# A two-layer hybrid encoder on one core: how its norms are cut, ordered and queued

## The chip, the core and the metric

The kernel runs on one NeuronCore of a Trainium2 chip. The core has five engines with a queue of instructions each: TensorE (PE: matmuls and transposes, with its weight loads listed as PEld), VectorE (DVE), ScalarE (ACT), GpSimd (POOL) and SyncE (SP, which here only issues DMAs). Each engine takes its own instructions in a fixed order; semaphores hold an instruction back until what it reads is written. SBUF is the working memory, PSUM holds what PE writes, in banks of 512 fp32 columns. The metric is the time of one execution on the device, in microseconds (us).

## The reference

A sequence of 256 tokens with 1024 features goes through two layers and a final RMSNorm, all in float32. Each layer is

```
mod = silu(c) @ ada_w + ada_b                 -> sh_m, sc_m, g_m, sh_f, sc_f, g_f
h   = rms_norm(x, norm_mix_g) * (1 + sc_m) + sh_m
proj = h @ w_in                               -> three attention branches and three gates
merged = sigmoid(ga) * (o_na @ w_br_na) + sigmoid(gb) * (o_mla @ w_br_mla) + sigmoid(gc) * (o_gqa @ w_br_gqa)
x   = x + g_m * (merged @ w_out)
h   = rms_norm(x, norm_ffn_g) * (1 + sc_f) + sh_f
gate, up = split(h @ ffn_w_gate_up)
x   = x + g_f * ((silu(gate) * up) @ ffn_w_down)
```

with `rms_norm(x, g) = x * rsqrt(mean(x*x) + 1e-6) * g`. The branches are a neighbourhood attention, a latent attention (its query projection is w_uq) and a grouped-query attention.

## The kernel before, in words

**Tiles.** The 256 tokens are two tiles of 128 (t = 0 and 1). Weights stream from HBM; every matmul has a 128x128 block of the transposed activation as its stationary operand and up to 512 columns of a weight as its moving one.

**Two parts.** An fp32 value is split into a rounded part (hi, or whi for weights) and a residual (lo, wlo). `split_to` (L186) does it: ACT casts to the rounded part (L187), DVE subtracts it from the source (L188). A product is then three matmuls: hi x whi (L268), hi x wlo (L269) and lo x whi (L270).

**Items.** The program's work on PE is a list of items. An item is 256 rows of a weight (two chunks of 128, `nk` = 2) and 512 columns or fewer; `load_split` (L241) loads it on SP and splits it on ACT and DVE, into one of seven pairs of split weights (`spl`) through one of five raw buffers (`rawp`). Its matmuls are six for each tile. `group` (L254) makes the items of one weight slice: the first opens a PSUM accumulation, the last one's `post` function reads the sum.

**Order.** The main loop (L902) goes through the items. The first twelve run both tiles at once, in regions that fix PE's order as written (L918). From then on tile 0 runs an item as soon as it comes, and tile 1 follows LAG = 4 items behind, out of the list `pend` (L926). At the places in `flush` all of tile 1's pending items run before the list goes on, as the following stage needs the complete row of x. `step` (L896) counts the executed items; `later(k, f)` runs f that many steps later, and so puts PE's transposes behind other matmuls. `side` holds other work for given items: loads and sums for `mod` (L143), biases, attention.

Within an engine the order is not wholly that of the program text: a planner orders ready instructions by priority, and priority is by default the place in the text.

**A norm.** There are three such places: before each layer's FFN (`iF`, one per layer) and before the second layer's projection (`i0`). `post_res` (L696) takes half a row (cg = 0 or 1, 512 columns) of one tile: DVE multiplies the sum by the gate (L702) and adds it to x (L703), ACT sums the squares (L192). After the second half `norm` (L223) follows for that tile: `x_rstd` (L195) adds the two sums and EPS on POOL (L197) and raises to the power -0.5, also on POOL (L108); `x_scaled` (L200) scales both halves of x on DVE (L202). DN = 4 steps later the deferred part runs: `transposed` (L205) transposes four chunks of 128 columns into one PSUM bank (L209), and `modulate` (L212) makes of each chunk `A * x + B` on ACT (L218), then the rounded part on ACT (L187) and the residual on DVE (L188). The next stage's matmuls of that tile read them as hi and lo. The first norm of all is another function, `first_x` (L825), with the same `x_rstd`; after the last layer `after_ffn` (L770) uses `x_rstd` and writes the output.

Of the kernel before, what the change touches and what calls it, by code (L numbers as in the profile page):

```python
# [15 lines left out]
P = 128  # L16
# [10 lines left out]
LAG = 4  # L27
# [5 lines left out]
DN = 4  # L33
# [3 lines left out]
def encoder_kernel(ctx: ExitStack, tc: tile.TileContext, x, consts, cols, rows, ada_b, rpb, ada_w, w_in,  # L37
# [152 lines left out]
    def sumsq(t, hf, ss):  # L190
        junk = t2([P, 512])
        nc.scalar.activation(junk, x_sb[:, t, hf * 512:(hf + 1) * 512], AF.Square, scale=1.0 / 32.0,  # L192
                             accum_out=ss[:, hf:hf + 1])

    def x_rstd(t, ss):  # L195
        ms = sm(1)
        nc.gpsimd.tensor_scalar(out=ms, in0=ss[:, 0:1], scalar1=ss[:, 1:2], scalar2=EPS, op0=ALU.add, op1=ALU.add)  # L197
        return rstd_of(ms, 1)
# [13 lines left out]
    def modulate(t, kc0, n, xT, A, B, hT):  # L212
        full = t2([P, 512])
        fv = full.rearrange("p (j q) -> p j q", j=4)
        for j in range(n + 1):
            if j < n:
                kc = kc0 + j
                nc.scalar.activation(fv[:, j, :], xT[:, j, :], AF.Identity, scale=A[:, kc:kc + 1], bias=B[:, kc:kc + 1])  # L218
            if j >= 1:
                kc = kc0 + j - 1  # L220
                split_to(hT[0][:, kc, t * P:(t + 1) * P], hT[1][:, kc, t * P:(t + 1) * P], fv[:, j - 1, :])

    def norm(t, ss, A, B, hT):  # L223
        r = x_rstd(t, ss)
        xs = [x_scaled(t, r, hf) for hf in range(2)]

        def b_():
            for hf in range(2):
                modulate(t, hf * 4, 4, transposed(xs[hf]), A, B, hT)
# [24 lines left out]
    def group(units_src, nkc, n, lhs, post, bank=None):  # L254
# [3 lines left out]
        for u in range(nu):  # L258
            nk = min(2, nkc - 2 * u)

            def mm(t, it, u=u, nk=nk):
# [3 lines left out]
                for j in range(nk):  # L265
                    kc = 2 * u + j
                    first, last = kc == 0, kc == nkc - 1
                    nc.tensor.matmul(ps[t][:, 0:n], lhs(t, 0, kc), hi[:, j, 0:n], start=first, stop=False)  # L268
                    nc.tensor.matmul(ps[t][:, 0:n], lhs(t, 0, kc), lo[:, j, 0:n], start=False, stop=False)  # L269
                    nc.tensor.matmul(ps[t][:, 0:n], lhs(t, 1, kc), hi[:, j, 0:n], start=False, stop=last)  # L270
# [13 lines left out]
    flush = set()  # L284
    cur = [0]
# [18 lines left out]
    def new_ss(key):  # L304
        ssn[key] = {t: smp.tile([P, 2], F32, tag="ss", name=nm("ss")) for t in range(NT)}
# [3 lines left out]
    def layer(l):  # L309
# [341 lines left out]
        flush.add(i0)  # L651
        at(i0 + (7 if l == 0 else 0), params)
# [43 lines left out]
        def post_res(key, m, after, half=None):  # L696
            def f_(cg):
                def f(t, ps):
# [3 lines left out]
                    nc.vector.tensor_tensor(out=y, in0=ps, in1=G, op=ALU.mult)  # L702
                    nc.vector.tensor_tensor(out=xa, in0=xa, in1=y, op=ALU.add)  # L703
                    if key not in ssn:
                        new_ss(key)
                    sumsq(t, cg, ssn[key][t])
# [17 lines left out]
        flush.add(iF)  # L724

# [98 lines left out]

    def first_x():  # L825
# [76 lines left out]
    for i, it in enumerate(items):  # L902
# [10 lines left out]
        if i < 12:  # L913
# [4 lines left out]
            with tc.manual_schedule(engines={mybir.EngineType.PE}):  # L918
# [7 lines left out]
        if len(pend) >= LAG:  # L926
# [74 lines left out]
```

## Time and profile before

| what | us |
|---|---|
| median of 3 runs | 822.37 (821.83 to 822.97) |
| the profiled execution | 822.51 |
| its span, first to last instruction | 820.4 |
| PE busy | 790.7 |
| DVE busy | 598.8 |
| ACT busy | 453.7 |
| POOL busy | 25.8 |
| mean granted clock of PE | 0.991 |

A view lists what the hardware profiler saw in one execution. A line names the source line, the engine, the operation, what it writes <- what it reads, shapes and a count. Matmuls are pipelined: one is listed with 0.39 us but the next starts before its end, so that the distance of two starts tells the rate. "Idle before" is the time in which the engine did nothing just before, and the name behind the arrow is what it waited for last.

### The profile page before, as it was taken

What the parts mean: (1) busy time and instruction counts of PE and PEld (TensorE: products, weight loads), DVE (VectorE), ACT (ScalarE), POOL (GpSimd) and SP (SyncE); (2) the same over time, 40 slices, a digit from 0 to 9 for tenths busy, and PEclk for the clock granted to TensorE, in tenths of its full rate; (3) what the DMA queues carried; (4) which work ended last, traced back from release to release, by engine and by line L of the source; (5) the groups of instructions that cost most, each with busy time, mean ns of one, the idle gap of its engine ahead of it and who ended that gap; (6) DMA issues with size and microseconds to landing.
All of it is one profiled execution on the core that took longest, in us unless ns stands there. A gap on an engine that the chain in (4) does not pass through costs nothing.

```text
span 820.4 us, 10803 instructions
## 1 busy us (share of the span) xinstructions
PE 790.7 (96%) x3776; PEld 633.4 (77%) x3776; DVE 598.8 (73%) x955; ACT 453.7 (55%) x788; POOL 25.8 (3%) x40
## 2 busy tenths in 40 slices
PE   5998999999999999999999999999999999999996
PEld 3786776788878888888878877777887888888884
DVE  3369898789777888875667699878978666665462
ACT  4365887644485444443466687774448544444441
POOL 1002100000000000000000020000000000000000
PEclk9999999999999999999999999999999999999998
DMA  9979488697667989886874668778765677876631
GB/s 315 359 245 273 131 293 252 198 311 227 194 180 241 322 294 306 276 264 190 210 213 137 180 192 279 222 230 283 250 198 182 219 233 223 259 226 184 182 103 52
DMA packets 113414, 187.20 MB, mean 228 GB/s; under 512 B 14672, under 2 KB 34256, under 8 KB 113360
## 3 DMA queue, kind: packets, MB, share of 16 engines
q1 hardware_dynamic: 113360, 186.51, 73.1%
q8 instruction: 30, 0.49, 0.3%
q14 instruction: 24, 0.20, 0.1%
HBM read 185.44 MB, written 1.05 MB: 227 GB/s over the span
## 4 chain that ended last, share of the span: by engine, by line
issue 49%; PE 31%; DVE 8%; DMA 6%; ACT 4%; POOL 1%; POOLq 0%; DVEq 0%; ACTq 0%
PE mm L268 8%; PE mm L270 8%; PE mm L269 8%; DMA raw<-in_ada_w_dram 6%; DVE wlo L188 2%; DVE acc L140 2%; PE tp L861 1%; POOL sm L108 1%; PE o L629 1%; ACT P L587 1%; ACT tm L218 1%; DVE sm L574 1%; PE tp L209 1%; PE tp L608 1%; PE tp L560 1%
## 5 line engine op out<-in xcount | busy, mean ns | idle before, releaser
L188 DVE TENSOR_TENSOR wlo<-raw,whi 128x1024 fp32r<-128x1024 f32 (+2 forms) x248 | 298.3, 1209 | 115.0 <-ACT whi L187 114.8
L187 ACT CAST whi<-raw 128x1024 fp32r<-128x1024 f32 (+2 forms) x248 | 256.9, 1041 | 221.6 <-PE mm L270 137.1
L268 PE MATMUL mm<-whi,hi 128*128 128x512 f32 (+1 forms) x784 | 314.0, 400 | 1.8 <-ACT hi L882 1.1
L270 PE MATMUL mm<-whi,lo 128*128 128x512 f32 (+1 forms) x784 | 307.1, 392 | 0.2
L269 PE MATMUL mm<-wlo,hi 128*128 128x512 f32 (+1 forms) x784 | 306.1, 390 | 0.5 <-DVE wlo L188 0.4
L268 PEld LDWEIGHTS mm<-whi,hi 128*128 128x128 f32 x784 | 148.1, 189 | 34.7 <-issue 5.7
L270 PEld LDWEIGHTS mm<-whi,lo 128*128 128x128 f32 x784 | 147.7, 188 | 32.8 <-DVE lo L188 1.8
L269 PEld LDWEIGHTS mm<-wlo,hi 128*128 128x128 f32 x784 | 148.3, 189 | 28.9 <-DVE wlo L188 1.7
L140 DVE SCALAR_TENSOR_TENSOR acc<-raw,sc,acc 128x512 f32<-128x512 f32 x140 | 104.9, 749 | 32.2 <-DMA raw<-in_ada_w_dram 30.5
L270 PE MATMUL mm<-whi,s 128*128 128x512 f32 (+1 forms) x188 | 73.3, 390 | 2.4 <-DVE s L188 2.4
L268 PE MATMUL mm<-whi,s 128*128 128x512 f32 (+1 forms) x188 | 74.2, 395 | 0.4 <-ACT s L187 0.4
L269 PE MATMUL mm<-wlo,s 128*128 128x512 f32 (+1 forms) x188 | 73.1, 389 | 0.0
L270 PEld LDWEIGHTS mm<-whi,s 128*128 128x128 f32 x188 | 35.4, 189 | 9.8 <-DVE s L188 2.6
L268 PEld LDWEIGHTS mm<-whi,s 128*128 128x128 f32 x188 | 35.3, 188 | 7.9 <-ACT s L187 0.9
L269 PEld LDWEIGHTS mm<-wlo,s 128*128 128x128 f32 x188 | 35.4, 188 | 6.8
L592 ACT ACTIVATE P<-P,sm 128x256 f32<-128x256 f32 x64 | 29.3, 509 | 5.7 <-DVE sm L590 5.6
L587 ACT ACTIVATE P<-tp,sm,rq 128x256 f32<-128x256 f32 x32 | 17.8, 561 | 15.9 <-DVE sm L584 15.8
L197 POOL TENSOR_SCALAR sm<-ss 128x1 f32<-128x1 f32 x10 | 4.0, 404 | 662.4 <-ACT tm L192 662.4
L218 ACT ACTIVATE tm<-tp,cm,cm 128x128 f32<-128x128 f32 x48 | 21.3, 472 | 6.2 <-PE tp L209 6.2
L108 POOL TENSOR_TENSOR sm<-sm,nhalf 128x1 f32<-128x1 f32 (+2 forms) x22 | 18.4, 835 | 127.1 <-DVE sm L370 65.2
L192 ACT ACTIVATE tm<-x_sb 128x512 f32<-128x512 f32 x20 | 12.6, 632 | 16.8 <-DVE x_sb L703 14.6
L733 DVE TENSOR_TENSOR tm<-tm,mm 128x512 f32<-128x512 f32 (+1 forms) x24 | 15.4, 640 | 8.7 <-PE mm L270 7.1
(157 smaller groups left out, 637.7 us busy)
## 6 DMA issues: line engine op xcount, KB each, us to landing
raw<-in_ada_w_dram SPq DMA_DIRECT2D x80, 512.0 KB, 4.8
raw<-in_w_gu_dram SPq DMA_DIRECT2D x80, 512.0 KB, 4.6
raw<-in_w_in_dram SPq DMA_DIRECT2D x64, 512.0 KB, 4.6
raw<-in_w_dn_dram SPq DMA_DIRECT2D x44, 512.0 KB, 4.8
s<-in_ada_w_dram SPq DMA_DIRECT2D x32, 256.0 KB, 6.7
raw<-in_w_out_dram SPq DMA_DIRECT2D x16, 512.0 KB, 4.9
raw<-in_w_in_dram SPq DMA_DIRECT2D x16, 256.0 KB, 5.0
raw<-in_w_gqa_dram SPq DMA_DIRECT2D x8, 512.0 KB, 5.6
```

What stands on the lines that cost most here:

```text
L108: nc.gpsimd.tensor_tensor(out=r, in0=ms, in1=nhalf[:, 0:n], op=ALU.pow)
L140: nc.vector.scalar_tensor_tensor(out=acc, in0=raw[:, j, :], scalar=sc[:, kc:kc + 1], in1=acc, op0=ALU.mult, op1=ALU.add)
L187: nc.scalar.copy(hi_ap, src)
L188: nc.vector.tensor_tensor(out=lo_ap, in0=src, in1=hi_ap.bitcast(F32), op=ALU.subtract)
L192: nc.scalar.activation(junk, x_sb[:, t, hf * 512:(hf + 1) * 512], AF.Square, scale=1.0 / 32.0, accum_out=ss[:, hf:hf + 1])
L218: nc.scalar.activation(fv[:, j, :], xT[:, j, :], AF.Identity, scale=A[:, kc:kc + 1], bias=B[:, kc:kc + 1])
L268: nc.tensor.matmul(ps[t][:, 0:n], lhs(t, 0, kc), hi[:, j, 0:n], start=first, stop=False)
L269: nc.tensor.matmul(ps[t][:, 0:n], lhs(t, 0, kc), lo[:, j, 0:n], start=False, stop=False)
L270: nc.tensor.matmul(ps[t][:, 0:n], lhs(t, 1, kc), hi[:, j, 0:n], start=False, stop=last)
L587: nc.scalar.activation(pt[:, t, :], src[:, t, :], AF.Exp, bias=nb[:, t:t + 1], scale=scale[t], accum_out=rs[:, t:t + 1])
L592: nc.scalar.activation(pt[:, t, :], pt[:, t, :], AF.Copy, scale=rc[:, t:t + 1])
L733: nc.vector.tensor_tensor(out=hd[:, 0:n], in0=sgv, in1=up, op=ALU.mult)
```

## The change

- `sumsq` adds EPS to the first half's sum on DVE; `x_rstd` then adds the second half's on DVE. POOL keeps the power.
- `modulate`: for the first half (chunks 0 to 3) ACT writes the rounded part straight from the transposes, and DVE computes the same `A * x + B` from the transposes on its own and subtracts. For chunks 4 to 7 ACT computes and casts as before, chunk by chunk.
- The steps of `norm`, of `modulate` and of the second half of `post_res` are given high priority: the planner treats them as if they stood at the start of the program.
- DN goes from 4 to 5, and around the three norms (`norm_at`) tile 1 follows five items behind and not four, from one item before the flush to five after it.
- In `group` the six matmuls of an item and tile run as hi x whi for both chunks, hi x wlo for both, lo x whi for both.
- In the first twelve items `issue_after` queues each region's PE instructions behind the last one before it.

```diff
--- before.py
+++ after.py
@@ -30,7 +30,7 @@
 DH = 10
 DM = 4
 DG = 4
-DN = 4
+DN = 5
 
 
 @with_exitstack
@@ -191,10 +191,12 @@
         junk = t2([P, 512])
         nc.scalar.activation(junk, x_sb[:, t, hf * 512:(hf + 1) * 512], AF.Square, scale=1.0 / 32.0,
                              accum_out=ss[:, hf:hf + 1])
+        if hf == 0:
+            nc.vector.tensor_scalar_add(ss[:, 2:3], ss[:, 0:1], EPS)
 
     def x_rstd(t, ss):
         ms = sm(1)
-        nc.gpsimd.tensor_scalar(out=ms, in0=ss[:, 0:1], scalar1=ss[:, 1:2], scalar2=EPS, op0=ALU.add, op1=ALU.add)
+        nc.vector.tensor_tensor(out=ms, in0=ss[:, 1:2], in1=ss[:, 2:3], op=ALU.add)
         return rstd_of(ms, 1)
 
     def x_scaled(t, r, hf):
@@ -212,21 +214,29 @@
     def modulate(t, kc0, n, xT, A, B, hT):
         full = t2([P, 512])
         fv = full.rearrange("p (j q) -> p j q", j=4)
-        for j in range(n + 1):
-            if j < n:
-                kc = kc0 + j
+        for j in range(n):
+            kc = kc0 + j
+            hi, lo = (hT[p][:, kc, t * P:(t + 1) * P] for p in range(2))
+            if kc0 == 0:
+
+                nc.scalar.activation(hi, xT[:, j, :], AF.Identity, scale=A[:, kc:kc + 1], bias=B[:, kc:kc + 1])
+                nc.vector.tensor_scalar(out=fv[:, j, :], in0=xT[:, j, :], scalar1=A[:, kc:kc + 1],
+                                        scalar2=B[:, kc:kc + 1], op0=ALU.mult, op1=ALU.add)
+            else:
                 nc.scalar.activation(fv[:, j, :], xT[:, j, :], AF.Identity, scale=A[:, kc:kc + 1], bias=B[:, kc:kc + 1])
-            if j >= 1:
-                kc = kc0 + j - 1
-                split_to(hT[0][:, kc, t * P:(t + 1) * P], hT[1][:, kc, t * P:(t + 1) * P], fv[:, j - 1, :])
+                nc.scalar.copy(hi, fv[:, j, :])
+            nc.vector.tensor_tensor(out=lo, in0=fv[:, j, :], in1=hi.bitcast(F32), op=ALU.subtract)
 
     def norm(t, ss, A, B, hT):
-        r = x_rstd(t, ss)
-        xs = [x_scaled(t, r, hf) for hf in range(2)]
+        with tc.high_priority():
+            r = x_rstd(t, ss)
+            xs = [x_scaled(t, r, hf) for hf in range(2)]
 
         def b_():
             for hf in range(2):
-                modulate(t, hf * 4, 4, transposed(xs[hf]), A, B, hT)
+                xT = transposed(xs[hf])
+                with tc.high_priority():
+                    modulate(t, hf * 4, 4, xT, A, B, hT)
 
         later(DN, b_)
 
@@ -262,12 +272,12 @@
                 if u == 0:
                     ps[t] = bank(t) if bank else psmm.tile([P, 512], F32, tag="mm", name=nm("mm"))
                 hi, lo = it["w"]
-                for j in range(nk):
-                    kc = 2 * u + j
-                    first, last = kc == 0, kc == nkc - 1
-                    nc.tensor.matmul(ps[t][:, 0:n], lhs(t, 0, kc), hi[:, j, 0:n], start=first, stop=False)
-                    nc.tensor.matmul(ps[t][:, 0:n], lhs(t, 0, kc), lo[:, j, 0:n], start=False, stop=False)
-                    nc.tensor.matmul(ps[t][:, 0:n], lhs(t, 1, kc), hi[:, j, 0:n], start=False, stop=last)
+
+                for n_, (part, w) in enumerate(((0, hi), (0, lo), (1, hi))):
+                    for j in range(nk):
+                        kc = 2 * u + j
+                        nc.tensor.matmul(ps[t][:, 0:n], lhs(t, part, kc), w[:, j, 0:n], start=(kc == 0 and n_ == 0),
+                                         stop=(kc == nkc - 1 and n_ == 2))
 
             pf = None
             if u == nu - 1:
@@ -282,6 +292,7 @@
 
     side = {}
     flush = set()
+    norm_at = []
     cur = [0]
     deferred = []
 
@@ -302,7 +313,7 @@
     ssn = {}
 
     def new_ss(key):
-        ssn[key] = {t: smp.tile([P, 2], F32, tag="ss", name=nm("ss")) for t in range(NT)}
+        ssn[key] = {t: smp.tile([P, 3], F32, tag="ss", name=nm("ss")) for t in range(NT)}
         return ssn[key]
 
 
@@ -649,6 +660,8 @@
             at(s + (k * span) // nseq, f)
 
         flush.add(i0)
+        if l > 0:
+            norm_at.append(i0)
         at(i0 + (7 if l == 0 else 0), params)
         at(i0 + (12 if l == 0 else 8), na_bias)
 
@@ -699,11 +712,14 @@
                     G = mods[(l, m)][:, cg * 512:(cg + 1) * 512]
                     xa = x_sb[:, t, cg * 512:(cg + 1) * 512]
                     y = t2([P, 512])
-                    nc.vector.tensor_tensor(out=y, in0=ps, in1=G, op=ALU.mult)
-                    nc.vector.tensor_tensor(out=xa, in0=xa, in1=y, op=ALU.add)
                     if key not in ssn:
                         new_ss(key)
-                    sumsq(t, cg, ssn[key][t])
+                    with ExitStack() as pri:
+                        if cg == 1:
+                            pri.enter_context(tc.high_priority())
+                        nc.vector.tensor_tensor(out=y, in0=ps, in1=G, op=ALU.mult)
+                        nc.vector.tensor_tensor(out=xa, in0=xa, in1=y, op=ALU.add)
+                        sumsq(t, cg, ssn[key][t])
                     if cg == 1:
                         after(t)
                     elif half:
@@ -722,6 +738,7 @@
             group(kslice(w_out[l], cg * 512, 512), 8, 512, mlhs, pr(cg))
         iF = len(items)
         flush.add(iF)
+        norm_at.append(iF)
 
 
         st["hid"] = {}
@@ -821,6 +838,9 @@
     for l in range(L):
         layer(l)
     xT0 = {}
+
+    def last_pe():
+        return next(i for i in reversed(nc.cur_bb.bb.instructions) if i.engine == mybir.EngineType.PE)
 
     def first_x():
         xT = act.tile([P, KC, S], F32, tag="lo", name=nm("xT"))
@@ -915,7 +935,7 @@
             q1 = i // 3 + 1
             if i % 3 == 1 and q1 < 4:
                 raws = first_loads(q1)
-            with tc.manual_schedule(engines={mybir.EngineType.PE}):
+            with tc.issue_after(last_pe()), tc.manual_schedule(engines={mybir.EngineType.PE}):
                 if i % 3 == 1 and q1 < 4:
                     four = first_sums(q1, raws)
                 if i % 3 == 2 and q1 < 4:
@@ -923,7 +943,8 @@
                 step(0, i)
                 step(1, i)
             continue
-        if len(pend) >= LAG:
+        lag = LAG + 1 if any(b - 1 <= i < b + 6 for b in norm_at) else LAG
+        while len(pend) >= lag:
             step(1, pend.pop(0))
         step(0, i)
         pend.append(i)
```

## Rows read from the trace of the kernel before

**Rows 1.** The page, part 1: busy us (share of the span) xinstructions of each engine

```profile
PE 790.7 (96%) x3776; PEld 633.4 (77%) x3776; DVE 598.8 (73%) x955; ACT 453.7 (55%) x788; POOL 25.8 (3%) x40
```

**Rows 2.** The list of waits of PE, whole span: us in total, times, longest us

```profile
PE tp L209 <- DVE tm L202: 11.9, 7, 7.8
PE mm L270 <- DVE s L188: 2.4, 1, 2.4
```

**Rows 3.** Timeline of PE in the first norm: start us, us, what, count, idle before

```profile
226.07 0.39 PE L270 MATMUL mm<-whi,lo 128*128 128x512 f32 x1
...
230.38 0.39 PE L268 MATMUL mm<-whi,hi 128*128 128x512 f32 x1
231.72 1.07 PE L209 MATMUL tp<-con,tm 128*128 128x128 f32 x8 [0.95 <-DVE tm L202]
232.54 0.48 PE L269 MATMUL mm<-wlo,hi 128*128 128x512 f32 x1
...
233.56 0.40 PE L270 MATMUL mm<-whi,lo 128*128 128x512 f32 x1
...
234.02 0.39 PE L269 MATMUL mm<-wlo,hi 128*128 128x512 f32 x1
234.50 0.50 PE L270 MATMUL mm<-whi,lo 128*128 128x512 f32 x1
...
238.48 0.39 PE L269 MATMUL mm<-wlo,hi 128*128 128x512 f32 x1
239.21 1.06 PE L209 MATMUL tp<-con,tm 128*128 128x128 f32 x8 [0.34 <-DVE tm L202]
```

**Rows 4.** Timeline of PE in the second norm, between the layers

```profile
421.90 0.39 PE L270 MATMUL mm<-whi,s 128*128 128x512 f32 x1
423.12 1.07 PE L209 MATMUL tp<-con,tm 128*128 128x128 f32 x8 [0.83 <-DVE tm L202]
...
425.18 0.39 PE L270 MATMUL mm<-whi,s 128*128 128x512 f32 x1
...
430.01 0.35 PE L270 MATMUL mm<-whi,lo 128*128 128x416 f32 x1
430.99 1.06 PE L209 MATMUL tp<-con,tm 128*128 128x128 f32 x8 [0.63 <-DVE tm L202]
432.70 0.46 PE L268 MATMUL mm<-whi,hi 128*128 128x416 f32 x1 [0.65 <-ACT hi L187]
```

**Rows 5.** Timeline of DVE in the first norm

```profile
226.48 1.22 DVE L188 TENSOR_TENSOR wlo<-raw,whi 128x1024 fp32r<-128x1024 f32 x1
227.61 0.68 DVE L702 TENSOR_TENSOR tm<-mm,G 128x512 f32<-128x512 f32 x1
...
231.09 0.88 DVE L202 TENSOR_SCALAR tm<-x_sb,sm 128x512 f32<-128x512 f32 x2 [0.87 <-POOL sm L108]
```

**Rows 6.** Timelines of POOL and, last line, of ACT in the first norm

```profile
229.88 0.51 POOL L197 TENSOR_SCALAR sm<-ss 128x1 f32<-128x1 f32 x1 [141.36 <-ACT tm L192]
230.48 0.58 POOL L108 TENSOR_TENSOR sm<-sm,nhalf 128x1 f32<-128x1 f32 x1
...
232.39 0.81 ACT L218 ACTIVATE tm<-tp,cm,cm 128x128 f32<-128x128 f32 x2 [0.72 <-PE tp L209]
```

**Rows 7.** Timeline of POOL at the end of the kernel

```profile
814.94 0.30 POOL L197 TENSOR_SCALAR sm<-ss 128x1 f32<-128x1 f32 x1 [4.55 <-ACT tm L192]
```

**Rows 8.** Groups of instructions by line: busy us, mean ns of one, idle before

```profile
L218 ACT ACTIVATE tm<-tp,cm,cm 128x128 f32<-128x128 f32 x48 | 21.3, 472 | 6.2 <-PE tp L209 6.2
...
L188 DVE TENSOR_TENSOR lo<-tm,hi 128x128 fp32r<-128x128 f32 x48 | 12.2, 289 | 3.2 <-ACT hi L187 3.0
...
L370 DVE TENSOR_SCALAR sm<-sm 128x2 f32<-128x2 f32 x4 | 0.7, 164 | 0.0
```

**Rows 9.** Timeline of PE in the first item

```profile
18.57 0.72 PE L269 MATMUL mm<-wlo,hi 128*128 128x416 f32 x1 [0.37 <-DVE wlo L188]
```

**Rows 10.** Windows: busy of PE, PEld, DVE, ACT, POOL; PEclk, DMA share, GB/s

```profile
78.00:82.00 4.00, 4.00 (x17) 3.02 (x16) 4.00 (x13) 1.79 (x5) 0.00 (x0) 0.57 0.60 172
```

## Prediction

> **What bounds the kernel now.** The page comes first: TensorE (PE) is busy 790.7 of 820.4 us, and DVE, the next, 598.8 [rows 1]. PE takes its instructions in a fixed order, one after the other, so a change pays only where PE stands still. The list of PE's waits says where: the transposes of L209 wait for the scaled activations of L202, 11.9 us in 7 places, 7.8 of them the start of the kernel; next is a single wait of 2.4 us for a residual of L188 [rows 2]. That leaves 4.1 us in six places: two tiles in each of three norms.
>
> PE's timeline shows each place by starts (the idle in its brackets counts from modelled ends, so it is less). A 512-column matmul follows the one before after 0.227 us ((230.38 - 226.07) / 19). In the first norm tile 0's last matmul starts at 226.07; the one at 230.38 should be followed at 230.61, and the transposes start at 231.72: 1.11 us lost. At 234.50 a matmul with the residual comes 0.25 late; at 239.21 tile 1's transposes come 0.51 late. Sum 1.87 [rows 3]. The third norm, from 621, repeats these three steps. In the second, between the layers, tile 0's transposes at 423.12 are 0.99 late and tile 1's at 430.99 0.80 (its matmuls there have 416 columns, 0.19 apart); then the rounded part of tile 1 is missing: 432.70 is 1.71 after 430.99, of which eight transposes with their matmul behind take 0.82 to 0.9 as in rows 3, so 0.81 lost. Sum 2.60 [rows 4]. All three: 1.87 + 2.60 + 1.87 = 6.3 us, the most that the norms can give but for steps of 0.1.
>
> **What makes the transposes late** is a chain over four engines. Tile 0's sum is complete some 0.4 us after 226.07, when DVE has just begun a weight split of 1.22; L702 gets its turn at 227.61, 1.1 late, and the two L202 at 231.09 [rows 5]. Between them lie the square sum on ACT and, on POOL, L197 at 229.88 and L108 at 230.48, 0.60 apart [rows 6]. From last matmul to transposes that is 5.65 us, and tile 1 takes the same 5.65 (233.56 to 239.21, rows 3).
>
> **The change, part by part**, summed against the profiled execution, 822.51 us (span 820.4 and 2.1 around it), 0.14 above the median of 822.37.
>
> *Five items (DN, lag).* Between tile 0's last matmul and its transposes stand three items now, 18 matmuls; with five held back it is four items, 24. The transposes are then due 25 x 0.227 = 5.67 us after 226.07, against a chain of 5.65. So the first wait of each norm goes even if the chain gets no faster: 1.11 + 0.99 + 1.11 = 3.2. Likewise four items of tile 0 instead of three and a part cover tile 1's chain, and 0.51 + 0.51 go. In the second norm those four are 416 wide: 0.23 + 24 x 0.19 = 4.8 against 5.81 (425.18 to 430.99); 1.0 must come from a shorter chain there. The 0.81 goes as well: one more item of tile 0, 6 x 0.227 = 1.36, now stands between tile 1's transposes and its first matmul. What moves is one item of tile 1 per norm, behind tile 0's last. In the first and third norm it ends tile 1's first half, so its L702, L703 and square sum move too; they become ready 1.36 after tile 0's L702 and don't hold it up. No DMA is added or moved in SP's order; a pair of split weights, and with it the next load's place, comes free one item later (rival two).
>
> *Priority and rstd.* L702 ahead of the split gains up to 1.1 per chain. L197, 0.51 on POOL there and 0.30 at the end of the kernel [rows 7], becomes a DVE instruction like L370, 0.16 [rows 8], and POOL's L108 then waits for DVE and not for ACT. I take 0.15 saved; the bounds are 0 (the hop to POOL eats it) and 0.35. The add of EPS is another 0.16 on DVE, ten times, while ACT squares the second half; weight splits queue behind it that are not due yet. Together these give the second norm its 1.0; I count the 0.80. At the end the 0.15 lies on the last chain and counts in full. At the start the same saving leads to sums that read loads still on their way: zero taken, 0.15 at best.
>
> *Rounded part straight from the transposes.* For chunks 0 to 3 the separate cast on ACT goes, and hi is there after one L218, 0.47. DVE gets four instructions more per tile, put at the 0.29 of its 128x128 subtract [rows 8]: 6 x 4 x 0.29 = 7.0 us of DVE work beside PE. Its cover is that DVE is idle 27% of the span; with that gone it delays splits (rival two). The modulate steps also go ahead of splits.
>
> *Residual products last.* The same products in another order, each with its own weight load as now: no cost. An item asks for wlo as third matmul instead of second, and for the first residual as fifth instead of third, 0.45 later, which is more than the 0.25 at 234.50; that goes twice. The second hi is asked for 0.45 earlier, and below it is in time. Two places outside the norms gain. The first item waits 0.37 for wlo at 18.57 [rows 9]; the second hi product now runs there (0.35 taken; zero if loads then wait). In the wait of 2.4 at w_uq [rows 2] two products go ahead (0.2 taken, since DVE's queue sets the end; 0 to 0.35).
>
> *issue_after* keeps the first twelve items in the order in which they run already: nothing.
>
> Sum: of the norms' 6.3 I take 5.7, leaving 0.1 per tile for small waits; with 0.15 at the end, 0.35 and 0.2 that is 6.4. **822.5 - 6.4 = 816.1 us.** With all terms at their bounds this case spans 815.0 to 817.5 (five items alone: 3.2 + 1.0 + 0.8).
>
> **A rule against the change.** Today ACT alone reads a bank of transposes, two L218 in 0.81, so 0.34 apart [rows 6]. After the change ACT and DVE both read it, neither needing the other's result; no row before shows such a pair. Without turns a chunk takes those 0.34; with turns 0.47 + 0.29 + two hops of 0.03 (POOL's end at 231.06 to 231.09) = 0.82. ACT starts 0.67 after the transposes (231.72 to 232.39), so with turns the fourth hi is ready at 0.67 + 3 x 0.82 + 0.47 = 3.6. PE wants it after 0.82 + 1.36 + 1.36 + 0.3 = 3.8. Either way it is in time, by 0.2 at least, and the sum stays. The Trainium skill (PSUM — Partial Sum Buffer, section PSUM bank collisions raise a hardware error) bears on this: two engines may not touch one bank in the same partitions at once, reads included, so that software has to put them in turn. By that rule the fourth hi comes at 3.6; no run yet shows it.
>
> **The rivals.** *One: turns with splits in the gaps; slower.* An engine that waits for its turn may take a weight split, 1.22, instead of some 0.4 of waiting: 0.8 late per split. One per tile costs 0.8 - 0.2 = 0.6; two cost 1.4, on six tiles 8.4: 824.5. It makes the kernel slower from two splits per tile on. For it: a split that has begun is not interrupted, as at 227.61. Against it: the steps have priority. 10%.
>
> *Two: weights late; about the same.* Six items then hold six of the seven split pairs, and DVE does norm work first. If one wlo still runs when PE wants it, 1.22 less 0.2 of cover, at each of six tiles, 6.0 come back: 822.1. Against it: while the five held-back items run, 6.8 us, PE uses no new pair, time for five splits. 12%.
>
> *Three: the order does not come out as written.* Only the first twelve items have a fixed order on PE. Elsewhere the planner moves work: the matmul at 230.38 has been put ahead of the transposes that stand before it in the program. Done more widely, that moves the wait from L209 to hi, and half of the 5.7 stays: 819.0. 13%.
>
> *Four: the clock.* After the wait at w_uq the granted clock reads 0.57 for 4 us, the 1.2 GHz level for most of them [rows 10]: 4 x 0.43 = 1.7 lost. If the wait becomes so short that it does not fall, 814.4; with half of the wait gone too, 813.2. 8%.
>
> **Numbers.** The forecast has 57%. From 813.0 to 820.4 the range takes in rivals four and three (with three quarters staying); one and two stay out, 22%. A measurement of this kernel tells 0.2%, 1.6 us, from no change. Faster: 0.57 + 0.13 + 0.08 = 0.78; same 0.12 (two); slower 0.10 (one).
>
> **What would show it.** Right: L209 waits for L202 at the start alone; the transposes follow a matmul after 0.23 at all six places; L702 starts within 0.1 of tile 0's sum; hi of the first four chunks 0.34 or 0.82 apart, which tells about the turns. Wrong: PE waits for hi (one, three) or wlo (two) in the norms, the clock falls in a new place, or PE loses time in the attention stages, whose order may shift with the products.

## The result: slower, and the profile after

The changed kernel takes **829.55 us** (median of 4 runs, 827.26 to 830.59) against 822.67 for the kernel before on the same chip: ratio 1.0071, 95% interval 1.0049 to 1.0093. It is slower; 816.1 was forecast, with 10% for slower. The profiled execution is the run of 827.26, the fastest of the four, with a span of 825.6 and a mean granted clock of 0.991; the other three have 0.987 to 0.990, so part of what the median loses beyond this trace is clock.

First the engines, part 1 of the page, as in [rows 1]:

```profile
PE 790.9 (96%) x3776; PEld 633.4 (77%) x3776; DVE 608.4 (74%) x999; ACT 449.9 (54%) x764; POOL 21.9 (3%) x30
```

PE does the same work at the same mean clock (0.991 in both), so nearly all of this execution's loss is standstill. DVE has 9.6 us more, ACT 3.8 less, POOL 3.9 less.

Next the list of PE's waits (us in total, times, longest us), beside [rows 2]:

```profile
PE tp L211 <- DVE ss L195: 7.8, 1, 7.8
PE mm L279 <- ACT hi L222: 5.2, 3, 2.1
PE mm L279 <- DVE s L188: 3.5, 1, 3.5
PE mm L279 <- DVE lo L228: 1.6, 3, 0.8
...
PE tp L211 <- DVE tm L204: 0.3, 1, 0.3
```

The transposes (L209 before, L211 now) wait at the start of the kernel and, after it, only 0.3 in all: that part did what it says. In their place stand waits for the rounded part (L222) and the residual (L228), and the wait at w_uq has grown from 2.4 to 3.5.

Where the time went is read by counting PE's instructions: both kernels have 3776 in nearly the same order, so the start of the n-th in the one trace less that in the other tells how far the kernel is behind there. The differences between two such points, in us against the kernel before (minus is a gain; one profiled execution each; the last column is the whole span, with the stretches between the columns in it):

| PE instructions | 0-300 start | 300-1000 w_uq, attention | 1000-1200 norm 1 | 1900-2100 norm 2 | 2900-3050 norm 3 | end |
|---|---|---|---|---|---|---|
| changed kernel | -0.94 | +0.41 | +2.99 | +1.52 | +1.97 | +5.16 |
| e6, direct part alone | -1.08 | +0.36 | +4.01 | +3.59 | +4.03 | +10.38 |
| e5, five items alone | +0.58 | -0.18 | +1.62 | -1.17 | 0.00 | -0.08 |
| e1, cast kept | +0.09 | +0.09 | +3.48 | -0.60 | +2.43 | +3.71 |
| e2, one reader | -0.47 | +0.58 | +1.58 | -0.98 | +0.58 | +1.00 |
| e8, one reader, square behind | -0.60 | +0.64 | -0.91 | -1.20 | -0.66 | -2.99 |

The first column does not tell what the parts are worth: e6 changes nothing at the start and gains 1.08 there. The granted clock from 16 to 24 us is 0.57 in the kernel before and 0.79 in e6, e9, e10 and the changed kernel, with either order of products.

The norms, which should have given 5.7, cost 6.5. Their first one, in the timeline of PE (start us, us, what, count, idle before), against [rows 3]:

```profile
229.40 0.62 PE L279 MATMUL mm<-whi,lo 128*128 128x512 f32 x2
229.86 1.04 PE L211 MATMUL tp<-con,tm 128*128 128x128 f32 x8
230.65 0.71 PE L279 MATMUL mm<-whi,hi 128*128 128x512 f32 x2
...
232.12 0.61 PE L279 MATMUL mm<-whi,hi 128*128 128x512 f32 x2
234.82 0.50 PE L279 MATMUL mm<-whi,hi 128*128 128x512 f32 x1 [2.08 <-ACT hi L222]
...
237.34 0.50 PE L279 MATMUL mm<-whi,lo 128*128 128x512 f32 x1 [0.41 <-DVE lo L228]
```

Tile 0's transposes follow their matmul without a pause. One item later, at 232.12, PE does two products with the first hi, its item's and one that the planner pulled ahead from the next group, and stands 2.08 us for the second. What ACT did in that time, from its timeline, against [rows 6]:

```profile
231.05 0.45 ACT L222 ACTIVATE hi<-tp,cm,cm 128x128 fp32r<-128x128 f32 x1
232.40 0.63 ACT L192 ACTIVATE tm<-x_sb 128x512 f32<-128x512 f32 x1 [0.89 <-DVE x_sb L721]
...
233.03 1.03 ACT L187 CAST whi<-raw 128x1024 fp32r<-128x1024 f32 x1
233.97 0.45 ACT L226 ACTIVATE tm<-tp,cm,cm 128x128 f32<-128x128 f32 x1
234.32 0.44 ACT L222 ACTIVATE hi<-tp,cm,cm 128x128 fp32r<-128x128 f32 x1
...
237.27 0.44 ACT L222 ACTIVATE hi<-tp,cm,cm 128x128 fp32r<-128x128 f32 x1
239.52 0.81 ACT L222 ACTIVATE hi<-tp,cm,cm 128x128 fp32r<-128x128 f32 x2 [1.81 <-PE tp L211]
```

And what DVE did, against [rows 5]:

```profile
230.49 1.22 DVE L188 TENSOR_TENSOR wlo<-raw,whi 128x1024 fp32r<-128x1024 f32 x1
231.62 0.68 DVE L721 TENSOR_TENSOR x_sb<-x_sb,tm 128x512 f32<-128x512 f32 x1
232.23 1.22 DVE L188 TENSOR_TENSOR wlo<-raw,whi 128x1024 fp32r<-128x1024 f32 x1
233.36 0.40 DVE L223 TENSOR_SCALAR tm<-tp,cm,cm 128x128 f32<-128x128 f32 x1
```

Two things lie between the first hi (231.05) and the second (234.32). One is the **square** of tile 1's first half (L192): ACT takes its queue in order and stands 0.89 for the addition to x (L721; the expectations call it the residual), which DVE does between two weight splits. The other is a **turn**: L223 reads the same bank, in the kernel's order between two L222, and DVE comes to it at 233.36, behind those splits. The turn is over at 233.76, but ACT is then busy with a weight (L187) and has a chunk of the second half (L226) ahead of the second hi, both put there by the planner. The third hi starts at 237.27; of the pair at 239.52 one is tile 0's fourth, the other belongs to tile 1. That ACT does wait for DVE there, and DVE for ACT, is in the view by source line; for L222:

```profile
its engine sat idle before it (us, times) until:
  PE tp L211: 4.2, 3
  DVE tm L223: 2.6, 3
who waited for it (us, times):
...
  PE mm L279: 5.2, 3
  DVE tm L223: 4.1, 2
```

DVE's new instruction L223 needs no result of L222 nor L222 one of L223; they share the bank alone. Its price is in the groups by line, beside [rows 8]:

```profile
L222 ACT ACTIVATE hi<-tp,cm,cm 128x128 fp32r<-128x128 f32 x24 | 10.6, 455 | 6.8 <-PE tp L211 4.2 <-DVE tm L223 2.6
...
L223 DVE TENSOR_SCALAR tm<-tp,cm,cm 128x128 f32<-128x128 f32 x24 | 9.7, 405 | 4.1 <-ACT hi L222 4.1
```

### The profile page after: what moved, and what is told of

The parts are those of the page before. It is cut to its first block, busy times and chain, and to the rows that moved or that the text cites. A ratio compares the mean times of both kernels' runs of the same rounds, so it can differ in the third digit from the quotient of the medians.

```text
span 825.6 us, 10808 instructions
## 1 busy us (share of the span) xinstructions
PE 790.9 (96%) x3776; PEld 633.4 (77%) x3776; DVE 608.4 (74%) x999; ACT 449.9 (54%) x764; POOL 21.9 (3%) x30
## 3 DMA queue, kind: packets, MB, share of 16 engines
HBM read 185.44 MB, written 1.05 MB: 226 GB/s over the span
## 4 chain that ended last, share of the span: by engine, by line
PE 77%; DVE 9%; DMA 5%; ACT 4%; issue 3%; POOL 1%; SPq 0%; POOLq 0%; DVEq 0%; ACTq 0%
PE mm L279 68%; DMA raw<-in_ada_w_dram 4%; DVE wlo L188 3%; PE o L640 1%; PE tp L571 1%; PE tp L757 1%; DVE acc L140 1%; PE tp L619 1%; ACT whi L187 1%; PE tp L881 1%; DMA s<-in_ada_w_dram 1%; POOL sm L108 1%; ACT P L598 1%; DMA con<-in_consts_dram 1%; PE tp L122 1%
## 5 line engine op out<-in xcount | busy, mean ns | idle before, releaser
L187 ACT CAST whi<-raw 128x1024 fp32r<-128x1024 f32 (+2 forms) x248 | 257.2, 1041 | 219.2 <-PE mm L279 142.7
L279 PE MATMUL mm<-whi,hi 128*128 128x512 f32 (+1 forms) x784 | 252.6, 401 | 6.7 <-ACT hi L222 5.2
L279 PE MATMUL mm<-whi,lo 128*128 128x512 f32 (+1 forms) x784 | 242.7, 390 | 1.6 <-DVE lo L228 1.6
L279 PE MATMUL mm<-wlo,hi 128*128 128x512 f32 (+1 forms) x784 | 243.3, 391 | 0.0
L279 PEld LDWEIGHTS mm<-whi,hi 128*128 128x128 f32 x784 | 141.6, 189 | 39.5 <-ACT hi L222 8.0
L279 PE MATMUL mm<-whi,s 128*128 128x512 f32 (+1 forms) x376 | 106.0, 393 | 4.5 <-DVE s L188 3.5
L279 PE MATMUL mm<-wlo,s 128*128 128x512 f32 (+1 forms) x188 | 58.2, 389 | 0.0
L598 ACT ACTIVATE P<-tp,sm,rq 128x256 f32<-128x256 f32 x32 | 17.7, 559 | 14.0 <-DVE sm L595 11.6
L767 ACT ACTIVATE tm<-mm 128x512 f32<-128x512 f32 x20 | 11.9, 597 | 21.4 <-PE mm L279 20.8
L192 ACT ACTIVATE tm<-x_sb 128x512 f32<-128x512 f32 x20 | 12.5, 627 | 17.7 <-DVE x_sb L721 15.5
L545 ACT ACTIVATE s<-mm 128x512 f32<-128x512 f32 x24 | 14.3, 598 | 11.4 <-PE mm L279 11.4
L720 DVE TENSOR_TENSOR tm<-mm,G 128x512 f32<-128x512 f32 x16 | 11.0, 687 | 11.1 <-PE mm L279 11.0
L619 PEld LDWEIGHTS tp<-con,P 128*128 128x128 f32 x128 | 15.0, 140 | 5.2 <-issue 2.3
```

Source lines behind the costliest of these rows:

```text
L187: nc.scalar.copy(hi_ap, src)
L279: nc.tensor.matmul(ps[t][:, 0:n], lhs(t, part, kc), w[:, j, 0:n], start=(kc == 0 and n_ == 0), stop=(kc == nkc - 1 and n_ == 2))
L545: nc.scalar.activation(st["gate"][gi][:, t, :], ps, AF.Tanh, scale=0.5)
L598: nc.scalar.activation(pt[:, t, :], src[:, t, :], AF.Exp, bias=nb[:, t:t + 1], scale=scale[t], accum_out=rs[:, t:t + 1])
L619: nc.tensor.transpose(tv[:, k, t * P:(t + 1) * P], pts[i][:, t, k * P:(k + 1) * P], ident)
L767: nc.scalar.activation(sg, ps, AF.Silu)
```

## The experiments

Every ratio is against the kernel before on the same chip, with its 95% interval. An edit adds or removes lines, so line numbers shift a little from kernel to kernel; the names stay.

**First four: undo one part each.** The theory then was the turns alone; rivals were the priority, the product order, and the six items.

e1 puts the old way to hi back, for all chunks:

```
-            if kc0 == 0:
-                nc.scalar.activation(hi, xT[:, j, :], AF.Identity, ...)
-                nc.vector.tensor_scalar(out=fv[:, j, :], in0=xT[:, j, :], ...)
+            if j < n: nc.scalar.activation(fv[:, j, :], xT[:, j, :], AF.Identity, ...)
+            if j >= 1: split_to(hi, lo, fv[:, j - 1, :])
```

> The changed kernel with the old way to the rounded part for all eight chunks (ACT writes the full value from the transposes, ACT rounds it, DVE subtracts), so that ACT alone reads a bank of transposes; five items, priority, rstd on DVE and product order stay. Theory (turns between ACT and DVE on the bank, with weight splits and other work standing between the turns): the norms' 6.5 us of loss become a gain, 816 to 818. Rival 1 (priority puts weight splits and the attention's steps in a worse order): it stays at 827 to 830. Rival 2 (product order: PE asks for the second hi earlier than it can come): 827 to 830 as well, or more, as hi then takes a cast longer. Rival 3 (six items hold the splits): 827 to 830.

Measured: 827.52, ratio 1.0065 (1.0041 to 1.0089). The theory of the turns alone fell: with one reader and no turns the norms still lose 5.3 (table). Its first norm shows why. ACT's timeline in e1:

```profile
233.11 0.63 ACT L192 ACTIVATE tm<-x_sb 128x512 f32<-128x512 f32 x1 [1.25 <-DVE x_sb L716]
...
233.74 1.49 ACT L220 ACTIVATE tm<-tp,cm,cm 128x128 f32<-128x128 f32 x4
235.11 0.50 ACT L187 CAST hi<-tm 128x128 fp32r<-128x128 f32 x2
```

The transposes began at 230.57, yet ACT stands 1.25 for the addition to x (L716) that the square reads, with the whole modulate behind it, and PE waits 2.48 for hi, until 235.46. In the kernel before that square ran at 226.59, ahead of the transposes at 231.72; the five items moved it.

e2 leaves hi straight from the transposes, but takes the full value by a second ACT read of the bank, so that ACT is its only reader:

```
-                nc.vector.tensor_scalar(out=fv[:, j, :], in0=xT[:, j, :], scalar1=A[:, kc:kc + 1],
-                                        scalar2=B[:, kc:kc + 1], op0=ALU.mult, op1=ALU.add)
+                nc.scalar.activation(fv[:, j, :], xT[:, j, :], AF.Identity, scale=A[:, kc:kc + 1], bias=B[:, kc:kc + 1])
```

> The rounded part still straight from the transposes for chunks 0 to 3, but the full value comes from a second ACT read of the same bank in place of the DVE instruction: no second reader, so no turns, and DVE loses four instructions per tile. Theory: 815 to 818, no wait of PE for hi over 0.5 in the norms. Rival 4 (not the turns but the direct form itself, which puts ACT's second pass or the reordered subtraction in the way): 824 to 830. Rivals 1 to 3: 827 to 830.

Measured: 822.16, 1.0001 (0.9990 to 1.0012). It lies between the theory's range and the rivals': 7.4 us come back, not all; of the waits for hi 3.5 us in four places stay.

e3 takes the three `tc.high_priority()` out; e4 puts the three products of a chunk together again.

> The changed kernel without the three places of priority; the direct part stays. Theory: the turns stay and splits still stand between them, if anything more of them: 826 to 832. Rival 1 (priority): 815 to 820.

> The changed kernel with the three products of a chunk together again. Theory: hi of the second chunk is asked for 0.45 later and its residual 0.45 earlier, the losses at the norms change by less than 2 us: 826 to 831. Rival 2 (product order): 815 to 820.

Measured: e3 824.62, 1.0026 (1.0011 to 1.0042), below the range of the theory and above that of its rival: beside turns and the moved square priority costs some 4 to 5 us (by the ratios and by the medians). e4 828.12, 1.0068 (1.0051 to 1.0085): the product order is not the cause.

**Next four: one part alone, and the square moved.** The new theory: the five items put the square of tile 1's first half ahead of tile 0's hi; the turns are a second loss beside it.

e5 is the kernel before with DN = 5, the longer lag, rstd on DVE and `issue_after` at the start:

> The kernel before with the five items and rstd on DVE alone (no priority, no direct part, old product order). New theory, from the traces of the first four runs: the five items move the residual and the first square of tile 1's first half behind tile 0's transposes, where ACT's queue has that square ahead of tile 0's hi, waiting for a residual that DVE does between two weight splits; the norms then lose by the move alone: 823 to 827, PE waiting some 2 us for hi in the first and third norm, none for the transposes. Rival (the move is harmless and the turns, the priority or the product order carry the loss; the prediction's own sum): 817 to 819.

Measured: 821.78, 0.9992 (0.9979 to 1.0005). The profile has both sides of it: PE waits for the transposes at the start alone, and for hi 3.6 us in two places:

```profile
PE tp L211 <- DVE tm L204: 8.0, 1, 8.0
PE mm L271 <- ACT hi L187: 3.6, 2, 1.8
```

What the transposes gained, hi gave back. As a rival to "the move is harmless" the theory holds; its range began 1.2 too high.

e6 is the kernel before with the direct part alone:

> The kernel before with the direct part alone (ACT writes hi from the transposes, DVE the full value from the same bank, for chunks 0 to 3). The square keeps its old place. Theory of the turns: an ACT and a DVE read alternate, a DVE read behind weight splits holds the next hi back, PE waits for hi or lo in the norms and the time is 824 to 828. Rival (turns cost nothing while the square is out of the way): 821 to 823.

Measured: **833.32, 1.0125** (1.0102 to 1.0149), beyond the range of the theory. The square has its old place here, so this is the direct part by itself. DVE's timeline in its first norm, whose transposes begin at 231.00:

```profile
231.16 2.35 DVE L188 TENSOR_TENSOR wlo<-raw,whi 128x1024 fp32r<-128x1024 f32 x2
233.44 0.40 DVE L221 TENSOR_SCALAR tm<-tp,cm,cm 128x128 f32<-128x128 f32 x1
233.87 0.29 DVE L226 TENSOR_TENSOR lo<-tm,hi 128x128 fp32r<-128x128 f32 x1
234.39 1.23 DVE L188 TENSOR_TENSOR wlo<-raw,whi 128x1024 fp32r<-128x1024 f32 x1 [0.23 <-ACT whi L187]
235.53 0.41 DVE L221 TENSOR_SCALAR tm<-tp,cm,cm 128x128 f32<-128x128 f32 x1
```

And ACT's:

```profile
231.67 0.46 ACT L220 ACTIVATE hi<-tp,cm,cm 128x128 fp32r<-128x128 f32 x1 [0.72 <-PE tp L209]
233.31 1.05 ACT L187 CAST whi<-raw 128x1024 fp32r<-128x1024 f32 x1 [1.18 <-PE mm L275]
234.26 0.45 ACT L220 ACTIVATE hi<-tp,cm,cm 128x128 fp32r<-128x128 f32 x1
```

DVE's first turn comes at 233.44, behind two splits; the next stands behind a third. ACT's rounding of a weight (L187) was put into the gap, where it waits 1.18 for PE to release a buffer. So the chunks come at 231.67 and 234.26 and not 0.82 apart, and PE waits eight times, 6.1 us, for lo:

```profile
PE mm L275 <- DVE lo L226: 6.1, 8, 1.1
```

After these waits PE's granted clock falls, in all three norms. The windows of e6 (busy of PE, PEld, DVE, ACT, POOL; PEclk, DMA share, GB/s):

```profile
232.00:236.00 4.00, 2.92 (x11) 1.52 (x9) 3.74 (x7) 2.82 (x8) 0.00 (x0) 1.00 0.72 227
236.60:240.00 3.40, 3.38 (x8) 2.06 (x8) 3.36 (x10) 1.93 (x6) 0.15 (x1) 0.50 0.64 199
...
434.60:438.00 3.40, 3.40 (x13) 3.17 (x13) 1.22 (x3) 0.09 (x1) 0.14 (x1) 0.50 0.60 174
636.00:639.30 3.30, 3.30 (x8) 2.41 (x9) 2.40 (x7) 0.72 (x2) 1.27 (x2) 0.50 0.24 89
```

Three stretches of 3.4 us at 0.50, the 1.2 GHz level, cost up to 1.7 each, 5.1 of the 11.6 us that the norms of this execution lose; the rest is standstill.

e7 is e1, and e8 is e2, with the square of tile 1's first half put behind tile 0's last modulate step in ACT's queue:

```
+                        moved = t == 1 and key != (L - 1, "n")
+                        if moved and cg == 1:
+                            with tc.issue_after(state["mod", 0]):
+                                sumsq(1, 0, ssn[key][1])
...
+                        if not (moved and cg == 0):
+                            sumsq(t, cg, ssn[key][t])
```

> The first run (cast kept) with one thing more: the square of tile 1's first half is put behind tile 0's last modulate step in ACT's queue. New theory: the wait of 2.5 us for hi in the first norm and its like in the third go, or fall below 0.5, and with them the half-clock stretches behind them: 820 to 823, from 827.5. Rival (priority, product order or six items holding splits carry the loss): 826 to 829.

> The second run (full value by a second ACT read, so one reader of the bank) with the square of tile 1's first half behind tile 0's modulate. New theory: the waits for hi of 1.5 and 0.3 in the first norm and their like in the third go; the norms then gain what the prediction said, 4 to 6 us against the kernel before, and what stays lost is the stage of w_uq: 817 to 819.5. Rival: 821 to 823, as without the move.

Measured: e7 824.45, 1.0017 (1.0003 to 1.0032), between its two ranges; the waits for hi went from 5.9 us in four places, the longest 2.5, to 3.8 in eight, the longest 0.6, and the norm's stretch at half clock (0.50 from 235.3 to 238.6 in e1) is gone. e8 **818.53, 0.9955 (0.9934 to 0.9975)**: faster than both kernels. Its first norm in PE's timeline:

```profile
229.97 0.62 PE L280 MATMUL mm<-whi,lo 128*128 128x512 f32 x2
230.43 1.04 PE L211 MATMUL tp<-con,tm 128*128 128x128 f32 x8
...
232.69 0.99 PE L280 MATMUL mm<-whi,hi 128*128 128x512 f32 x2
233.52 0.63 PE L280 MATMUL mm<-wlo,hi 128*128 128x512 f32 x2
```

The pair of products with the first and the second hi begins at 232.69 and the next follows 0.83 later, where a pair that waits for nothing takes 0.46 (229.97 to 230.43); in the changed kernel the product with the second hi alone starts 2.70 after that with the first. In the list of waits of e8 hi of L222 no longer stands.

**Four on what was left.**

e9 is the kernel before with e2's form of the direct part alone. e10 is the kernel before with the new product order alone. e11 is e8 with that order in the first twelve items only:

```
+                order = [(n_, j) for n_ in range(3) for j in range(nk)]
+                if items.index(it) >= 12:
+                    order = [(n_, j) for j in range(nk) for n_ in range(3)]
```

e12 is e11 without priority.

> The kernel before with the direct part alone as in run e6_direct_alone, but the full value comes from a second ACT read of the bank, so ACT is its only reader. Theory of the turns: the 10 us that e6_direct_alone lost are all in the wait of ACT for DVE's read behind weight splits, so 821 to 824 here. Rival (hi before the full value, or the residual one step later, is what PE waits for): 828 to 834.

> The kernel before with the residual products last in each item, alone. From the stages of the first runs: some 1 us gained at the start, some 2.3 lost in the stage of w_uq (a longer half-clock stretch there), part of it given back in the attention stage; norms within 0.5: 821 to 824.5. Rival (the order is free, or gains as predicted): 820 to 822.

> Run e8_one_reader_behind with the new product order in the first twelve items alone and the old one in all others. Theory (the order costs in the stage of w_uq what it gains at the start): 816 to 818. Rival (the norms of run e8 need the order, since the second hi comes late): 818.5 to 821.

> Run e11_order_first_twelve without the three places of priority. If priority itself costs something (run e3 against the changed kernel: 5 us less without it, turns present): 1 to 4 us below e11. If it only cost there by what it put between the turns: equal to e11 within 1, or up to 2 above, as the residual of tile 0 stands behind a split again.

Measured: e9 822.22, 1.0002 (0.9987 to 1.0018), 11.1 below e6. e10 822.37, 0.9999 (0.9986 to 1.0012): nothing in the end; it gains 1.05 up to the 300th instruction, as e6 does without the order, and loses 1.25 from there to the 1000th. e11 819.09, 0.9955 (0.9939 to 0.9971), and e12 819.81, 0.9958 (0.9943 to 0.9973): both equal to e8. e11 lies above the 816 to 818 expected and in the range of its rival, whose reason does not hold: its norms gain 2.9, e8's 2.8. So neither the order nor, with turns and square gone, the priority is worth anything that can be measured. That e11 would win back the loss at w_uq fell: its profiled execution loses 1.89 in that stage although the order there is the old one.

Why w_uq got slower is in e10's timelines, first ACT's, then DVE's:

```profile
73.73 1.04 ACT L187 CAST whi<-raw 128x1024 fp32r<-128x1024 f32 x1 [1.87 <-DMA raw<-in_w_in_dram]
74.68 0.85 ACT L187 CAST s<-tp 128x384 fp32r<-128x384 f32 x2
```

```profile
69.89 1.23 DVE L188 TENSOR_TENSOR wlo<-raw,whi 128x1024 fp32r<-128x1024 f32 x1 [0.78 <-ACT whi L187]
...
77.60 1.02 DVE L188 TENSOR_TENSOR s<-tp,s 128x384 fp32r<-128x384 f32 x2
```

The latent's rounded part (s) stands in ACT's queue behind a weight whose load has not landed; PE waits 3.46 for it. In the kernel before the same cast began at 72.72 with no load awaited ahead of it. But the wait that ends last is the one for the latent's residual on DVE, at 77.60, after which PE goes on at 78.21. In the changed kernel the cast begins at 72.32, no later than before, and yet the residual at 77.60 and PE at 78.20. In both a weight split stands at some 70 in DVE's queue and DVE waits 0.78 for it. The kernel before, without a split at that place, begins the residual at 76.54; e6, with the old order and 1.08 earlier on arrival, at 75.45. So it is not the early arrival that lengthens the stage, but what the planner puts ahead of the residual: from PE's 300th to its 400th instruction the ten kernels with the new order and 3776 instructions lose 1.4 to 3.3 us, and the four with the old one lose nothing. Part of it comes back in the attention stage behind. PE's clock goes with the loss: its mean from 74 to 86 is 0.86 in the six kernels with the old order in the first twelve items and 0.72 or 0.57 in the twelve with the new one. e11 shows that the order in those twelve is enough.

**Four more on what stayed open:** e2 and e9 had taken away the turns and DVE's instruction at once, and the shares of turns and square were not told apart. In e13 (the kernel before with the direct part) and e14 (the changed kernel) DVE keeps its instruction, but reads its own copy of the transposes in a second bank:

```
                 xT = transposed(xs[hf])
+                xT2 = transposed(xs[hf]) if hf == 0 else None
...
-                nc.vector.tensor_scalar(out=fv[:, j, :], in0=xT[:, j, :], scalar1=A[:, kc:kc + 1],
+                nc.vector.tensor_scalar(out=fv[:, j, :], in0=xT2[:, j, :], scalar1=A[:, kc:kc + 1],
```

e15 is the changed kernel with the square behind, e16 is e14 with the square behind.

> The kernel before with the direct part alone (as e6_direct_alone, 833.3), but the four transposes of chunks 0 to 3 are made twice, into two banks: ACT reads one, DVE the other. The DVE instruction stays where it was, no turns; PE does 24 transposes more, some 0.1 each, 2.5 us. Theory (turns): 822.2 of e9 plus 2.5, so 823 to 826.5. Rival (DVE's instruction behind splits makes the residual late): 829 to 835.

> The changed kernel with the same second copy of the transposes for DVE. The square stays ahead of most of the modulate. In ACT's queue all four hi then stand in one row ahead of it. Theory (turns): 820 to 825, with 2.5 of it for the added transposes, PE's waits for hi below 1 in total. Rival (DVE's instruction): 828 to 833, PE waiting for lo.

> The changed kernel with the square of tile 1's first half behind tile 0's modulate, turns left in. If turns and square add (7.4 and 3.6 us from the changed kernel over e2 to e8): 824.5 to 827.5. If they overlap (ACT waits for its turn anyway while the square runs): 827.5 to 830.

> The changed kernel with both: second bank for DVE, and the square behind the modulate. Theory: neither turns nor square are left, e8's 818.5 plus 2.5 for the transposes, 819 to 822.5. Rival (DVE's instruction): 825 to 831.

Measured: e13 822.86, 1.0008 (0.9994 to 1.0022), against 833.3 with one bank; e14 821.37, 0.9990 (0.9974 to 1.0006), against 829.55; e15 826.46, 1.0048 (1.0034 to 1.0061); e16 820.05, 0.9963 (0.9947 to 0.9980). e13 is 0.1 below its theory's range, the other three lie in theirs (e15 in that of turns and square that add). The second bank brings the time back although PE does 24 transposes more and DVE as much as before. Its ACT timeline in the first norm, e13:

```profile
231.36 1.50 ACT L220 ACTIVATE hi<-tp,cm,cm 128x128 fp32r<-128x128 f32 x4 [0.72 <-PE tp L209]
```

All four hi are done within 1.50. What is more, the queues themselves come out another way: without the turn the four stand in one row, with no weight between. And DVE's, e13, where L221 stands beside them and no longer between them:

```profile
231.99 0.72 DVE L221 TENSOR_SCALAR tm<-tp,cm,cm 128x128 f32<-128x128 f32 x2
```

So it is the shared bank, by the turns and by the order of the queues that comes with them. The four kernels of turns and square, medians in us:

| | square ahead of hi | square behind |
|---|---|---|
| turns (ACT and DVE read the bank) | 829.55 (changed kernel) | 826.46 (e15) |
| one reader | 822.16 (e2) | 818.53 (e8) |

By these medians the turns cost 7.4 and 7.9, the square 3.1 and 3.6, and they add up. By the ratios to the kernel before it is 0.70 and 0.93% for the turns, 0.23 and 0.46% for the square, where the changed kernel's ratio is known to 0.22%; so that they add up holds to some 2 us. The medians of the kernel before, in the five sets of runs, lie at 822.5 to 823.1.

## Why the prediction was wrong, step by step

- *Where PE stands still.* Right: the waits ahead of the transposes went with the five items (0.3 left in the changed kernel's list, none in e5's). What was not foreseen is what is late next.
- **The step that failed** is in "A rule against the change": "with turns the fourth hi is ready at 0.67 + 3 x 0.82 + 0.47 = 3.6 ... Either way it is in time, by 0.2 at least, and the sum stays". The durations were not far off (0.45 and 0.40 instead of 0.47 and 0.29), and the rule was right. The sum put the turns one behind the other, as if both queues held nothing else. Already the second hi began 4.5 us after the transposes (229.86 to 234.32), the third 7.4 and the fourth some 10. By a turn each engine's queue becomes part of the other's chain, and [rows 5] already had a split that made L702 1.1 late. The Trainium skill (PSUM — Partial Sum Buffer, section PSUM bank collisions raise a hardware error) asks for turns between two engines on one bank; the trace agrees, in the waits of L222 for L223 (2.6 us) and of L223 for L222 (4.1), and e13 shows that a second bank takes the cost away.
- *Rival one* named this mechanism and priced two splits per tile at 8.4 us, 824.5. Alone it costs 10.5 (e6), in the changed kernel 7.4 to 7.9. That the price came near is in part luck: it counts waits alone, and in e6 some 5 us are half clock. It was given 10%, since "the steps have priority". That was the wrong evidence: in the changed kernel two splits and an addition to x (L721, without priority) stand on DVE between the transposes and L223, with priority on the modulate.
- *Five items* held the second failing sentence: tile 1's L702, L703 and square "become ready 1.36 after tile 0's L702 and don't hold it up". That looked at DVE and at tile 0's sum. It left out ACT's queue, into which the square was moved ahead of tile 0's hi, and that the addition to x which it waits for has no priority. Worth 3.1 to 3.6.
- *Rivals two and three.* No wait for wlo stands in the changed kernel's list, so two fell. Of three, the planner did pull a product of the next group ahead of the second hi, but the wait that follows it is set by ACT and DVE; a share of its own was not measured.
- *DVE's instruction* was put at 0.29, from a subtraction in the rows; it took 0.40, but two in a row start 0.32 apart (e13), so 24 take some 7.7 us of DVE where 7.0 were taken. DVE's added busy time, 9.6, has the twenty small adds for EPS and rstd in it as well. Beside PE it cost nothing that can be measured: e13 has it and loses nothing.
- *Residual products last*, +0.35 and +0.2. The 0.37 of waiting for wlo in the first item does go, but no run shows a gain from it: e10's 1.05 at the start is also e6's. At w_uq, where 0.2 was to be gained, it costs 2.4 in e10 by the wait and the clock, of which 1.1 comes back up to the 1000th instruction; in sum nothing (e10). *Rival four* (the clock rises) went the other way there.
- *rstd on DVE*, 0.15 at the end: from PE's 3050th instruction to the end of the span the changed kernel gains 0.09 on the kernel before and e5 0.19 (of the kernels with it only e4 loses, 0.13); e6, with rstd on POOL, gains 0.00. Right.
- With turns and square gone, e8 stands at 818.5. Its norms gain 2.8 of the 5.7 in the profiled execution; some 3 us of gaps, each below 0.5, mostly ahead of lo and of transposes, are left there, and what sets them was not traced.

## What to carry to other kernels

Before a second engine is given the same PSUM bank to read, look at what stands in its queue at that place, not at the duration of its instruction: its whole backlog becomes a wait of the first engine, where one more read by the same engine, or a second copy, cost nothing measurable here. When an item is moved, follow each instruction that it issues into the queue of its engine and ask which instruction of the critical chain now stands behind it. Priority is no promise that the slots between two steps stay free, and a new order in one stage can put weight splits ahead of the critical chain in a later one.

## What was not expected of the hardware

- The same 128x128 is dearer on DVE from the bank of transposes with two scalars per partition (L223, 405 ns) than as a subtraction of two tiles in SBUF (L228, 283 ns); two in a row take 0.72 in e13, 0.32 apart.
- Waits of some 0.5 to 1.1 for lo, two or three in a norm, were followed by 3.4 us at the half clock in each of the three norms of e6, while in the profiled execution of the changed kernel a wait of 2.08 left the clock at 1.00 through that norm (222 to 252). Nor does the length of one wait decide: in e5 waits of 1.8 stand in the first and the third norm, and only in the first the mean clock falls, to 0.94 (222 to 252; 1.00 from 614 to 645). What does decide was not found. Small waits can cost as much again in clock as they do in standstill.
- Twenty-four more transposes, put at 2.5 us, showed less clearly than that: e13 is 0.6 above e9, e14 0.8 below e2, e16 1.5 above e8.
